# A hybrid encoder block on one core: the decay's bias moves to ScalarE, z is cut into quarter tiles among the keys, and the gating norm and spatial products go into the scans

## Chip, core and metric

The kernel runs on one core of a Trainium2 chip. The metric is device time in microseconds. A core has five instruction queues, each worked off in order: TensorE (PE, matmuls), VectorE (DVE), ScalarE (ACT), GpSimd (POOL) and SyncE (SP, which here issues most DMAs). They run beside each other and wait for each other by semaphores.

## What is computed

One layer on x, 1024 tokens by 1024 features, all in float32:

```python
x = x + 0.5 * swiglu(rmsnorm(x), ffn1)                   # 2816 hidden
p = rmsnorm(x) @ w_in                                    # u, v, q|k|v, z, b, a
y_a = gelu(u) * (W_s @ layernorm(gelu(v)) + b_s)         # 8 groups of 64, blocks of 128
q, k, v = split(silu(causal_conv4(qkv)))                 # 4 heads of 128, chunks of 64
decay = exp(where(tri, g_i - g_j, -inf))                 # g: cumulated in the chunk
L = strict(k_beta k^T * decay);  sol = (L + 1)^-1 [v_beta, k_beta e^g]
per chunk: v_new = u - w S;  o = q_dec S + attn v_new;  S = S e^gl + k_dec^T v_new
y_b = rmsnorm(o) * silu(z)
x = x + [y_a, y_b] @ w_out
x = x + 0.5 * swiglu(rmsnorm(x), ffn2);  y = rmsnorm(x)
```

## The kernel before

Matmuls keep float32's precision by splitting each operand into a high and a low part (`split`, L61 casts on ACT, L62 subtracts on DVE) and making three matmuls of it (`mm3`, L53). The two feed-forward parts form combinations of blocks (Strassen's way) on DVE and POOL. Between them lies the middle, in this order:

1. Token-major projections in token tiles of 128 (`token_steps`): eight contraction blocks, so 24 matmuls of 128x256 for a tile, into a PSUM bank `mm` (three of these), then an evacuation. First half of v (`v0`, spilled to DRAM), with the decay among it.
2. `decay(h)` for four heads: per head and half, `grb` is the row of cumulated g broadcast over partitions (a DMA), `gc` the same as a column. EL is exp(mask - grb + gc), EA is exp(grb - gc + mask), each 128x512 for four blocks of tokens: two operations on DVE (or POOL for half of EL), L900 to L905, then one Exp on ACT, L904 or L906.
3. `keys(h)`: projection and convolution of k (`proj_steps`: 24 matmuls of 128x512 into `mm` for each half, a copy to `pad` on ACT, L972, four operations on DVE, L974 and L976, a Silu on ACT, L978), then for each half four transposes (L947) and four products, L and the scaled keys to DRAM. `fill` runs two whole tiles of z's second half (`wz1`) behind each projection, 48 matmuls. There are two pads.
4. `substitute`: the 32x32 diagonal blocks of all chunks are inverted by forward substitution, 31 pairs of small DVE operations (L1023, L1025), the result X and its transpose Zb go to DRAM and are loaded again as Z and X.
5. Second half of v (`tm("v", 1, ev_v)`): gelu, layernorm (`mix`: two statistics operations on DVE, an add on DVE, a power on POOL, two scalings on DVE, L1180 to L1187), and, a pair of tiles later, `spatial`: eight matmuls of 128x128 into each of two `ax` banks, an add on DVE each (L1197).
6. Convolutions of blocks 8 and 0 (v and q of head 0), the first inverses, then eight scans of four steps each (`stage`), in which projections, inverses and queries of the next head fill PE (`weave`). Then u, the output projection, the last feed-forward part and the final norm.

A norm is one Square on ACT with a sum (L74), a multiply and add on DVE (L76), a power -0.5 on POOL (L70, `rpow`) and a scaling on DVE (L82). In the entries of the feed-forward parts its result is transposed by PE (L95) and combined (L118 and L119 casts and differences, with some L119 on POOL).

The order on each engine is not written out: a list scheduler with its own costs sets it when the program is built, by the order of the code and by what is ready. The number of buffers of each tile name limits how far it can go ahead; `tc.issue_after(ins)` holds instructions behind `ins` on their engine.

Of the kernel before, what the change touches and what calls it, by code (L numbers as in the profile page):

```python
# [30 lines left out]
def block_kernel(ctx: ExitStack, tc, a, out):  # L31
# [37 lines left out]
    def rpow(o, i, w):  # L69
        nc.gpsimd.tensor_tensor(o, i, half[:, :w], op=ALU.pow)  # L70

    def rstd_of(src, junk, n):
        ms = sm.tile([P, 1], F32, tag="ms", name="ms", bufs=4)
        nc.scalar.activation(junk, src, AF.Square, accum_out=ms)  # L74
        rs = sm.tile([P, 1], F32, tag="rs", name="rs", bufs=4)
        nc.vector.tensor_scalar(rs, ms, 1.0 / n, EPS, op0=ALU.mult, op1=ALU.add)  # L76
# [519 lines left out]
    with ExitStack() as f2:  # L596
# [150 lines left out]
        def fin(t, xt):  # L747
            o = gp.tile([P, D], F32, tag="gsp", name="o", bufs=8)
            if t < 7:
                normed(xt, st["gf"], o)  # L750
                nc.sync.dma_start(odram[t], o)
                return

            halves = slice(0, 512), slice(512, D)
# [26 lines left out]
def middle(tc, nc, a, L):  # L781
# [4 lines left out]
    bank, mm, mm3, split, rpow = L["bank"], L["mm"], L["mm3"], L["split"], L["rpow"]  # L786
# [4 lines left out]
    def K(i):  # L791
        return csa[:, i - 1]
# [95 lines left out]

    def decay(h):
        EL[h], EA[h] = (xp.tile([P, 2, 512], F32, tag="x", name="E") for _ in range(2))  # L890
        for hf in range(2):
            cs = slice(h * 8 + hf * 4, h * 8 + hf * 4 + 4)
            grb = lv.tile([P, 512], F32, tag="VT", name="grb", bufs=4)
            nc.sync.dma_start(grb, grd[:, cs.start * P:cs.stop * P].to_broadcast([P, 512]))
            lv_, av_ = v4(EL[h][:, hf]), v4(EA[h][:, hf])
# [6 lines left out]
            eng.tensor_tensor(lv_, mask(C_ML), v4(grb), op=ALU.subtract)
            eng.tensor_tensor(lv_, lv_, b4(gc[:, cs]), op=ALU.add)
            nc.scalar.activation(lv_, lv_, AF.Exp)  # L904
            nc.vector.tensor_tensor(av_, av_, mask(C_MA), op=ALU.add)  # L905
            nc.scalar.activation(av_, av_, AF.Exp)  # L906
# [81 lines left out]
    def keys(h, fill):  # L988
        kst = [kp.tile([P, 3, 512], F32, tag="kst", name="kst", bufs=3) for _ in range(2)]
        proj_conv(4 + h, [k[:, 0] for k in kst])  # L990
        for _ in range(2):
            next(fill, None)
        for hf in range(2):
            KT, kd, rw = (kst[hf][:, i] for i in range(3))
            cs = slice(h * 8 + hf * 4, h * 8 + hf * 4 + 4)
            kps = fourT(lambda t: KT[:, tl(t)])
            ssk = small("ssk")
            for t in range(4):
                nc.scalar.activation(rw[:, tl(t)], kps[:, tl(t)], AF.Square, accum_out=ssk[:, t:t + 1])
# [12 lines left out]
            nc.sync.dma_start(full(Ld, h * 2 + hf), v4(Lm))  # L1012

    def substitute():
        Lb = xp.tile([P, 32, 32], F32, tag="x", name="Lb")
        nc.sync.dma_start(Lb, diag(Ld))
        X = kp.tile([P, 32, 32], F32, tag="kst", name="X", bufs=3)
        nc.scalar.dma_start(X, a["i32"].to_broadcast([P, 1024]).rearrange("p (r c) -> p r c", r=32))
        tb = big("aT", 2)
        for j in range(31):  # L1020
            n, w = 31 - j, j + 1
            tv = tb[:, :n * w].rearrange("p (n w) -> p n w", w=w)
            nc.vector.tensor_tensor(tv, Lb[:, j + 1:, j:j + 1].to_broadcast([P, n, w]),  # L1023
                                    X[:, j:j + 1, :w].to_broadcast([P, n, w]), op=ALU.mult)
            nc.vector.tensor_tensor(X[:, j + 1:, :w], X[:, j + 1:, :w], tv, op=ALU.subtract)  # L1025
        nc.sync.dma_start(xz_d[0], X.rearrange("p r c -> p (r c)"))
        Z = xp.tile([P, 32, 32], F32, tag="x", name="Zb")
        nc.vector.tensor_copy(Z, X.rearrange("p r c -> p c r"))
# [174 lines left out]
    def ev_v(gm, later):  # L1203
        def f(t, ps):
            if t % 2 == 0:
                Vt[t // 2] = kp.tile([P, 2, 512], F32, tag="kst", name="vm", bufs=3)
                v = Vt[t // 2][:, :, 0:256]
                nc.sync.dma_start(v, sp["v"][t:t + 2, :, 0:256].rearrange("t p n -> p t n"))
                nc.scalar.activation(v, v, GELU)
            Vs = Vt[t // 2]  # L1210
            nc.scalar.activation(Vs[:, t % 2, 256:512], ps[:, :256], GELU)
            mix(t, Vs[:, t % 2], gm)
            if t % 2 == 1:
                for g in later:
                    g()
                later[:] = [partial(spatial, t, Vs, gm)]
        return f
# [77 lines left out]
    for h in range(HEADS):  # L1295
        x, y = H[h]
        if h + 1 < HEADS:
# [19 lines left out]
                wv = load_qkv(10 + h)  # L1317
            else:
                u0 = steps("u", 0, ev_u0, part=2)
            stage(x, weave(first(), queries(), (1,) + (2,) * 8), 2)  # L1320
            ny.load()
            if h + 2 < HEADS:
                wq_ = load_qkv(h + 2)
                more = proj_steps(10 + h, wv, values_of(h + 2))
            else:
                more = islice(u0, 16)
            stage(y, weave(second(), more, (1, 1, 2, 2, 2, 2, 2, 2, 2)), 2)
        else:
            stage(x, weave(chain(y.values(), y.queries()), islice(u0, 8), (0, 1, 1, 1, 0)), 1.5)
            stage(y, u0, 1)  # L1330
# [79 lines left out]
```

## Time and profile before

| | |
|---|---|
| median of three runs | 1840.59 us (1839.88 to 1841.27) |
| profiled execution, own time | 1839.26 us |
| its span | 1837.5 us |
| PE busy in the span | 1774.4 us, 97% |
| DVE, ACT, POOL busy | 1201.7, 694.2, 802.3 us |
| mean granted PE clock | 0.987 |

Views of the profile: the page gives busy time by engine; the list of waits gives what PE waited for; windows give busy time and PE's granted clock by stretch; a timeline gives each instruction or run of like instructions with its start, its duration, the idle time before it and what ended that (`[2.87 <-ACT pad L972]`); the list by lines groups instructions (count, busy us, mean ns, idle before). A name such as `pad<-mm` is what is written and what is read.

Stages by the clock of the span: first feed-forward part to about 640, keys of the four heads from 727 to 815, second half of v with the substitution from 815 to 895, scans from about 903, entry of the last feed-forward part at about 1185 to 1205.

### The profile page before, as it was taken

The page shows a single profiled execution, that of the slowest core. Times are in us where ns is not written, and L with a number is a line of the kernel's source. Part 1 is how long each engine was busy: PE and PEld are TensorE (multiplying, and loading weights), DVE is VectorE, ACT ScalarE, POOL GpSimd, SP SyncE. Part 2 cuts the span into 40 slices and gives each one's busy share as a digit, 9 for nine tenths or more (in the row PEclk, how much of TensorE's full clock was granted, in tenths as well). Part 3 has the DMA queues.
Part 4 walks back from the last instruction along what each step waited for, and adds up shares of the span by engine and source line. Part 5 has one row for each costly group of instructions (what it writes and reads, how often), then busy time and mean ns, then how long its engine had stood idle before and what let it go on. Part 6 is the DMA issues. An engine that isn't in the chain of part 4 may idle for free. (4 is left out here: it accounts for less than half of the span.)

```text
span 1837.5 us, 24764 instructions
## 1 busy us (share of the span) xinstructions
PE 1774.4 (97%) x9303; PEld 1498.3 (82%) x9303; DVE 1201.7 (65%) x1531; ACT 694.2 (38%) x1209; POOL 802.3 (44%) x627
## 2 busy tenths in 40 slices
PE   5999999999999999898999989989999999999997
PEld 4888888888888889797788978778888888888886
DVE  6867767655666585668755346797676766656546
ACT  6333233332434454332344543543333333243434
POOL 4656656665173013312132455386565665414001
PEclk8999999999999999999999999989999999999999
DMA  4254443454888554353432344324444445476744
GB/s 185 97 182 152 150 166 132 170 174 164 323 310 309 189 185 155 120 199 102 141 87 67 92 142 162 127 97 177 169 169 145 145 165 176 156 273 251 253 134 149
DMA packets 140552, 309.57 MB, mean 168 GB/s; under 512 B 27888, under 2 KB 42512, under 8 KB 140432
## 3 DMA queue, kind: packets, MB, share of 16 engines
q1 hardware_dynamic: 137936, 303.54, 47.9%
q10 hardware_dynamic: 2496, 4.44, 0.8%
q8 instruction: 73, 1.20, 0.3%
q14 instruction: 47, 0.39, 0.1%
HBM read 211.98 MB, written 95.96 MB: 168 GB/s over the span
## 5 line engine op out<-in xcount | busy, mean ns | idle before, releaser
L53 PE MATMUL mm<-unit 128*128 128x512 f32 x1056 | 242.9, 390 | 0.9 <-DVE unit L62 0.8
L53 PEld LDWEIGHTS mm<-unit 128*128 128x128 f32 x1056 | 197.6, 188 | 42.9 <-DVE unit L62 2.2
L62 DVE TENSOR_TENSOR gs<-s,gs 128x512 fp32r<-128x512 f32 x168 | 174.0, 1038 | 48.8 <-ACT gs L61 47.1
L61 ACT CAST gs<-s 128x512 fp32r<-128x512 f32 x168 | 104.1, 621 | 226.4 <-PE mm L53 111.2
L193 POOL TENSOR_TENSOR s<-graw 128x512 f32<-128x512 f32 x84 | 123.9, 1476 | 144.4 <-DMA graw<-in_f1gu_dram 112.2
L53 PE MATMUL ax<-T,gs 128*128 128x512 f32 x792 | 183.2, 389 | 0.0
L62 DVE TENSOR_TENSOR ga<-graw,ga 128x512 fp32r<-128x512 f32 x134 | 145.7, 1090 | 56.6 <-ACT ga L61 55.6
L53 PE MATMUL ax<-unit 128*128 128x512 f32 x792 | 180.5, 389 | 0.0
L53 PEld LDWEIGHTS ax<-T,gs 128*128 128x128 f32 x792 | 148.9, 188 | 31.0
L62 DVE TENSOR_TENSOR unit<-left,unit 128x1024 fp32r<-128x1024 f32 x84 | 106.8, 1272 | 103.0 <-ACT unit L61 103.0
L53 PEld LDWEIGHTS ax<-unit 128*128 128x128 f32 x792 | 148.7, 188 | 30.8
L53 PE MATMUL mm<-B,ga 128*128 128x512 f32 (+1 forms) x864 | 166.1, 346 | 3.8 <-ACT B L118 2.4
L53 PE MATMUL mm<-T,gs 128*128 128x512 f32 x720 | 166.4, 389 | 0.0
L53 PEld LDWEIGHTS mm<-B,ga 128*128 128x128 f32 x864 | 138.8, 192 | 24.0 <-ACT B L118 3.2
L53 PEld LDWEIGHTS mm<-T,gs 128*128 128x128 f32 x720 | 135.1, 188 | 28.1
L61 ACT CAST unit<-left 128x1024 fp32r<-128x1024 f32 x84 | 82.5, 982 | 191.2 <-PE ax L53 95.9
L53 PE MATMUL mm<-actT,wk 128*128 128x512 f32 x576 | 151.8, 405 | 0.0
L61 ACT CAST ga<-graw 128x512 fp32r<-128x512 f32 x134 | 83.1, 622 | 131.2 <-PE mm L53 46.0
L53 PE MATMUL ax<-B,ga 128*128 128x512 f32 x528 | 128.6, 393 | 1.7 <-DVE ga L62 1.7
L62 DVE TENSOR_TENSOR unit<-right,unit 128x1024 fp32r<-128x1024 f32 x84 | 111.2, 1324 | 27.0 <-ACT unit L61 27.0
L53 PE MATMUL mm<-wk,actT 128*128 128x256 f32 x960 | 123.8, 285 | 3.7 <-ACT pad L972 2.9
L70 POOL TENSOR_TENSOR rs<-rs,half 128x1 f32<-128x1 f32 (+1 forms) x29 | 19.4, 672 | 246.3 <-DVE rs L76 246.2
(252 smaller groups left out, 3125.0 us busy)
## 6 DMA issues: line engine op xcount, KB each, us to landing
left<-hq SPq DMA_DIRECT2D x70, 512.0 KB, 6.1
graw<-in_f1gu_dram SPq DMA_DIRECT2D x44, 512.0 KB, 5.6
wq<-t SPq DMA_DIRECT2D x44, 512.0 KB, 2.8
hq<-s SPq DMA_DIRECT2D x44, 512.0 KB, 3.1
graw<-in_f2gu_dram SPq DMA_DIRECT2D x44, 512.0 KB, 3.9
right<-wq SPq DMA_DIRECT2D x40, 512.0 KB, 4.6
wd<-in_f1wd_dram SPq DMA_DIRECT2D x22, 512.0 KB, 6.6
hq<-sg SPq DMA_DIRECT2D x22, 512.0 KB, 3.7
```

What stands on the lines that cost most here:

```text
L53: nc.tensor.matmul(*args, **kw)
L61: nc.scalar.copy(h, src)
L62: nc.vector.tensor_tensor(l, src, h, op=ALU.subtract)
L70: nc.gpsimd.tensor_tensor(o, i, half[:, :w], op=ALU.pow)
L193: nc.gpsimd.tensor_tensor(f, u, v, op=op)
```

## The change

- **Decay.** One operation adds the mask to (or takes from it) `grb`; gc, or its negative `ngc`, comes in as the bias of the Exp, a value per partition, so that each token block needs its own: 64 Exps of 128x128. Those of EL are written with the decay, those of EA behind the keys of their head. 14 of the 16 mask operations are on DVE, two on POOL.
- **z.** `part=4`: a tile of z is two steps of 12 matmuls. They stand ahead of the transposes of each half, in numbers by head and half.
- **Norms.** The multiply goes into the scale of the Square, the add to POOL, next to the power (`rsqrt`).
- **v.** `ev_v` only makes the gelu and stores it. `mixing` loads it, makes the layernorm (held behind the substitution's last operation, `solved`) and the spatial products, in steps that `beside` puts among the scans' fillers. Its constants have tiles of their own.
- **First convolutions.** Blocks 8 and 0 are held behind `solved`; their weights are loaded ahead of that.
- **Final norm.** Tile 6's scaling and store are deferred, the halves of the last tile exchanged.

```diff
+    def rsqrt(o, i, add, w=1):
+        nc.gpsimd.tensor_scalar(o, i, add, None, op0=ALU.add)
+        rpow(o, o, w)
...
-        nc.scalar.activation(junk, src, AF.Square, accum_out=ms)
+        nc.scalar.activation(junk, src, AF.Square, scale=n ** -0.5, accum_out=ms)
...
-        nc.vector.tensor_scalar(rs, ms, 1.0 / n, EPS, op0=ALU.mult, op1=ALU.add)
-        rpow(rs, rs, 1)
+        rsqrt(rs, ms, EPS)
...
+    ngc = na
+    nc.vector.tensor_scalar(ngc, gc, -1.0, None, op0=ALU.mult)
...
-            nc.vector.tensor_tensor(av_, v4(grb), b4(gc[:, cs]), op=ALU.subtract)
-            eng = nc.vector if hf else nc.gpsimd
-            eng.tensor_tensor(lv_, mask(C_ML), v4(grb), op=ALU.subtract)
-            eng.tensor_tensor(lv_, lv_, b4(gc[:, cs]), op=ALU.add)
-            nc.scalar.activation(lv_, lv_, AF.Exp)
-            nc.vector.tensor_tensor(av_, av_, mask(C_MA), op=ALU.add)
-            nc.scalar.activation(av_, av_, AF.Exp)
+            for e, i, eng, op in ((EL[h], C_ML, nc.gpsimd if hf == 0 and h < 2 else nc.vector, ALU.subtract), (EA[h], C_MA, nc.vector, ALU.add)):
+                eng.tensor_tensor(v4(e[:, hf]), K(i).unsqueeze(1).to_broadcast([P, 4, P]), v4(grb), op=op)
+
+    def exponents(e, bias, h):
+        for hf in range(2):
+            for t in range(4):
+                c = h * 8 + hf * 4 + t
+                nc.scalar.activation(e[h][:, hf, tl(t)], e[h][:, hf, tl(t)], AF.Exp, bias=bias[:, c:c + 1])
...
-        for _ in range(2):
-            next(fill, None)
         for hf in range(2):
+            for _ in range(((3, 3), (1, 3), (1, 2), (1, 2))[h][hf]):
+                next(fill, None)
...
-            rk = inv_norm(ssk, 1.0, EPS, "k")
+            rk = small("rk")
+            rsqrt(rk, ssk, EPS, 4)
...
+    def mixing(gm):
+        for t in range(0, 8, 2):
+            Vs = wp.tile([P, 2, 512], F32, tag="vm", name="vs", bufs=2)
+            nc.sync.dma_start(Vs, sp["v"][t:t + 2].rearrange("t p n -> p t n"))
+            for i in range(2):
+                with tc.issue_after(solved.ins):
+                    mix(t + i, Vs[:, i], gm)
+                yield
+            spatial(t + 1, Vs, gm)
+            yield
...
-    fill = token_steps([a["wz1"][0], a["wz1"][1]], 256, spill("z", 1), hT)
+    fill = token_steps([a["wz1"][0], a["wz1"][1]], 256, spill("z", 1), hT, part=4)
     for h in range(HEADS):
         keys(h, fill)
+        exponents(EA, ngc, h)
...
-    substitute()
+    solved = substitute()
     gm = gm_consts()
-    later = []
-    tm("v", 1, ev_v(gm, later))
+    tm("v", 1, ev_v)
+    w8, w0 = load_qkv(8), load_qkv(0)
...
+    def beside(steps):
+        for i, s in enumerate(steps):
+            if i in (1, 4, 7):
+                next(mixed, None)
+            yield s
...
-    proj_conv(8, values_of(0))
-    later.pop()()
-    proj_conv(0, queries_of(0))
+    with tc.issue_after(solved.ins):
+        together(proj_steps(8, w8, values_of(0)))
+        together(proj_steps(0, w0, queries_of(0)))
...
-            stage(x, weave(first(), queries(), (1,) + (2,) * 8), 2)
+            stage(x, weave(beside(first()), queries(), (1,) + (2,) * 8), 2)
...
-            stage(y, weave(second(), more, (1, 1, 2, 2, 2, 2, 2, 2, 2)), 2)
+            stage(y, weave(beside(second()), more, (1, 1, 2, 2, 2, 2, 2, 2, 2)), 2)
```

Three places show what the scheduler makes of it. The line numbers of the changed kernel are 4 to 12 higher than those of the kernel before. First, ACT in the keys of head 0: `E` are the decay's exponentials (in place), `wk` the weights' cast, `pad<-mm` the copy that frees PE's bank, `kst<-acc` the Silu of the keys. Before:

```order
L904 ACTIVATE E<-E 128x512 x2
L906 ACTIVATE E<-E 128x512
L836 COPY ev<-mm 128x256
L61 CAST wk<-raw 128x1024
L904 ACTIVATE E<-E 128x512
L906 ACTIVATE E<-E 128x512
L904 ACTIVATE E<-E 128x512
L906 ACTIVATE E<-E 128x512 x2
L972 COPY pad<-mm 128x512
L904 ACTIVATE E<-E 128x512
L978 ACT_TABLE_LOAD
L978 ACTIVATE kst<-acc 128x512
```

After, the same stretch and the next rows:

```order
L61 CAST wk<-raw 128x1024
L979 COPY pad<-mm 128x512
L913 ACTIVATE E<-E,na 128x128 x12
L985 ACT_TABLE_LOAD
L985 ACTIVATE kst<-acc 128x512
L979 COPY pad<-mm 128x512
L61 CAST wk<-raw 128x1024
L913 ACT_TABLE_LOAD
L913 ACTIVATE E<-E,na 128x128 x3
L1006 ACTIVATE kst,ssk<-ax 128x128 x4
L985 ACT_TABLE_LOAD
L985 ACTIVATE kst<-acc 128x512
```

The exponentials of EL (bias `gc`) are all ahead of these rows; those of EA (bias `na`, which holds `ngc`) stand around the copies and Silus of the keys, with a table load at each change between Exp and Silu. Second, DVE from the substitution's first operations on: `X<-X,aT` and `aT<-Lb,X` are the substitution, `vm` is v in its layernorm, `bst`, `bmv` and `brs` its statistics. Before:

```order
L1025 TENSOR_TENSOR X<-X,aT 128x29x3
L1197 TENSOR_TENSOR vm<-ax,bs 128x4x2x64
L1023 TENSOR_TENSOR aT<-Lb,X 128x112
L1180 BN_STATS bst<-vm 128x6
L1025 TENSOR_TENSOR X<-X,aT 128x28x4
L1182 BN_AGGR bmv<-bst 128x2
L1180 BN_STATS bst<-vm 128x6
L1023 TENSOR_TENSOR aT<-Lb,X 128x135
L1184 TENSOR_SCALAR brs<-bmv 128x1
L1186 SCALAR_TENSOR_TENSOR vm<-vm,bmv,rv 128x512
L1025 TENSOR_TENSOR X<-X,aT 128x27x5
L1187 SCALAR_TENSOR_TENSOR vm<-vm,brs,rv 128x512
```

After, at the substitution's end:

```order
L1031 TENSOR_TENSOR aT<-Lb,X 128x60
L1033 TENSOR_TENSOR X<-X,aT 128x2x30
L1031 TENSOR_TENSOR aT<-Lb,X 128x31
L1033 TENSOR_TENSOR X<-X,aT 128x31
L981 TENSOR_SCALAR acc<-pad,cw 128x512
L1036 COPY Zb<-X 128x1024
L983 SCALAR_TENSOR_TENSOR acc<-pad,cw,acc 128x512
L981 TENSOR_SCALAR acc<-pad,cw 128x512
L983 SCALAR_TENSOR_TENSOR acc<-pad,cw,acc 128x512 x4
L1192 BN_STATS bst<-vs 128x6
```

Layernorm, spatial adds and convolutions have left the substitution, in which only three `L62 TENSOR_TENSOR wk<-raw,wk` remain, and stand behind its last operation. Third, POOL at the entry of the last feed-forward part: `rs` is a norm's scale, `T` a combination's low part, `s` a sum of weights. Before:

```order
L119 TENSOR_TENSOR T_10404<-f,T_10404 128x4x128
L70 TENSOR_TENSOR rs<-rs,half 128x1 x3
L119 TENSOR_TENSOR T_10408<-f,T_10408 128x4x128
L119 TENSOR_TENSOR T_10708<-f,T_10708 128x4x128 x2
L193 TENSOR_TENSOR s_10734<-graw 128x512
L70 TENSOR_TENSOR rs<-rs,half 128x1
L193 TENSOR_TENSOR s_10736<-s_10734,graw 128x512
```

After:

```order
L74 TENSOR_SCALAR rs<-ms 128x1
L70 TENSOR_TENSOR rs<-rs,half 128x1
L163 TENSOR_TENSOR f<-f 128x512
L123 TENSOR_TENSOR T_10453<-f,T_10453 128x4x128
L74 TENSOR_SCALAR rs<-ms 128x1
L70 TENSOR_TENSOR rs<-rs,half 128x1
L74 TENSOR_SCALAR rs<-ms 128x1
L70 TENSOR_TENSOR rs<-rs,half 128x1
L123 TENSOR_TENSOR T_10449<-f,T_10449 128x4x128
L123 TENSOR_TENSOR T_10453<-f,T_10453 128x4x128
L123 TENSOR_TENSOR T_10753<-f,T_10753 128x4x128 x2
L197 TENSOR_TENSOR s_10779<-graw 128x512
```

The fourth power, which stood behind four rows of T and s, now stands ahead of them, next to its add.

More of the change, by code (lines that the diff above doesn't have):

```diff
@@ L749, in fin, with scaled @@
             if t < 7:
[L750 to L754, printed above, removed]
+                rs = rstd_of(xt, o, D)
+                def scaled():
+                    nc.vector.scalar_tensor_tensor(o, xt, rs, st["gf"], op0=ALU.mult, op1=ALU.mult)
+                    nc.sync.dma_start(odram[t], o)
+                if t == 6:
+                    return scaled
+                return scaled()
+            halves = slice(512, D), slice(0, 512)
             ms = sm.tile([P, 2], F32, tag="ms2", name="ms2")
@@ L757, in fin @@
             for i, f in enumerate(halves):
-                nc.scalar.activation(o[:, f], xt[:, f], AF.Square, accum_out=ms[:, i:i + 1])
+                nc.scalar.activation(o[:, f], xt[:, f], AF.Square, scale=D ** -0.5, accum_out=ms[:, i:i + 1])
             nc.gpsimd.tensor_tensor(rs, ms[:, 0:1], ms[:, 1:2], op=ALU.add)
-            nc.gpsimd.tensor_scalar(rs, rs, 1.0 / D, EPS, op0=ALU.mult, op1=ALU.add)
-            rpow(rs, rs, 1)
+            rsqrt(rs, rs, EPS)
             for f, eng in zip(halves, (nc.sync, nc.scalar)):
@@ L785, in middle @@
     hT, ident, sp, ba = L["hT"], L["ident"], L["sp"], L["ba"]
-    bank, mm, mm3, split, rpow = L["bank"], L["mm"], L["mm3"], L["split"], L["rpow"]
+    bank, mm, mm3, split, rpow, rsqrt = L["bank"], L["mm"], L["mm3"], L["split"], L["rpow"], L["rsqrt"]
     csa = kp.tile([P, NCONST - 1, P], F32, tag="kst", name="csa", bufs=3)
@@ L894, in decay @@
             nc.sync.dma_start(grb, grd[:, cs.start * P:cs.stop * P].to_broadcast([P, 512]))
-            lv_, av_ = v4(EL[h][:, hf]), v4(EA[h][:, hf])
-            def mask(i):
-                return K(i).unsqueeze(1).to_broadcast([P, 4, P])
-            nc.vector.tensor_tensor(av_, v4(grb), b4(gc[:, cs]), op=ALU.subtract)
-            eng = nc.vector if hf else nc.gpsimd
-            eng.tensor_tensor(lv_, mask(C_ML), v4(grb), op=ALU.subtract)
-            eng.tensor_tensor(lv_, lv_, b4(gc[:, cs]), op=ALU.add)
-            nc.scalar.activation(lv_, lv_, AF.Exp)
-            nc.vector.tensor_tensor(av_, av_, mask(C_MA), op=ALU.add)
-            nc.scalar.activation(av_, av_, AF.Exp)
+            for e, i, eng, op in ((EL[h], C_ML, nc.gpsimd if hf == 0 and h < 2 else nc.vector, ALU.subtract), (EA[h], C_MA, nc.vector, ALU.add)):
[5 more added lines that the diff above has]
+                nc.scalar.activation(e[h][:, hf, tl(t)], e[h][:, hf, tl(t)], AF.Exp, bias=bias[:, c:c + 1])
     Zt, Xt = [], []
@@ L1024, in substitute @@
                                     X[:, j:j + 1, :w].to_broadcast([P, n, w]), op=ALU.mult)
-            nc.vector.tensor_tensor(X[:, j + 1:, :w], X[:, j + 1:, :w], tv, op=ALU.subtract)
+            last = nc.vector.tensor_tensor(X[:, j + 1:, :w], X[:, j + 1:, :w], tv, op=ALU.subtract)
         nc.sync.dma_start(xz_d[0], X.rearrange("p r c -> p (r c)"))
@@ L1029, in substitute @@
         nc.sync.dma_start(xz_d[1], Z.rearrange("p r c -> p (r c)"))
+        return last
     class Half:
@@ L1163, in gm_consts, with const @@
     def gm_consts():
-        lng, lnb = big("rv", 2), big("rv", 2)
+        def const():
+            return wp.tile([P, 512], F32, tag="gmc", name="gmc", bufs=4)
+        lng, lnb = const(), const()
         nc.scalar.dma_start(lng, a["gm_ln_g"].to_broadcast([P, 512]))
@@ L1170, in gm_consts @@
         for i in range(2):
-            w = v4(big("u", 2))
+            w = v4(const())
             nc.scalar.dma_start(w, a["gmw"][:, i * 512:i * 512 + 512].rearrange("p (g n) -> p g n", g=4))
@@ L1201, in spatial, with ev_v @@
         nc.sync.dma_start(sp["m"][t - 1:t + 1].rearrange("t p n -> p t n"), Vs)
[L1203 to L1217, printed above, removed]
+    def ev_v(t, ps):
+        if t % 2 == 0:
+            Vt[t // 2] = kp.tile([P, 2, 512], F32, tag="kst", name="vm", bufs=3)
+            v = Vt[t // 2][:, :, 0:256]
+            nc.sync.dma_start(v, sp["v"][t:t + 2, :, 0:256].rearrange("t p n -> p t n"))
+            nc.scalar.activation(v, v, GELU)
+        nc.scalar.activation(Vt[t // 2][:, t % 2, 256:512], ps[:, :256], GELU)
+        if t % 2 == 1:
+            nc.sync.dma_start(sp["v"][t - 1:t + 1].rearrange("t p n -> p t n"), Vt[t // 2])
+    def mixing(gm):
[8 more added lines that the diff above has]
+            yield
     def ev_u0(t, ps):
@@ L1243, in middle @@
         decay(h)
+        exponents(EL, gc, h)
         together(islice(v0, 2))
-    fill = token_steps([a["wz1"][0], a["wz1"][1]], 256, spill("z", 1), hT)
+    fill = token_steps([a["wz1"][0], a["wz1"][1]], 256, spill("z", 1), hT, part=4)
     for h in range(HEADS):
         keys(h, fill)
+        exponents(EA, ngc, h)
     together(fill)
-    substitute()
+    solved = substitute()
     gm = gm_consts()
-    later = []
-    tm("v", 1, ev_v(gm, later))
+    tm("v", 1, ev_v)
+    w8, w0 = load_qkv(8), load_qkv(0)
     H = [[Half(h, hf) for hf in range(2)] for h in range(HEADS)]
@@ L1272, in weave @@
         yield from few
+    mixed = mixing(gm)
+    def beside(steps):
[3 more added lines that the diff above has]
+            yield s
     def stage(x, filler, rate):
```

## The prediction

> **What bounds the kernel now.** The page comes first: how long the span is and how much of it TensorE (PE) works.
>
> ```profile
> span 1837.5 us, 24764 instructions
> PE 1774.4 (97%) x9303; PEld 1498.3 (82%) x9303; DVE 1201.7 (65%) x1531; ACT 694.2 (38%) x1209; POOL 802.3 (44%) x627
> ```
>
> PE is busy 97% of the time, and the change takes no matmul away (it cuts some groups smaller and moves others). So it can only win what PE waits, about 60 us in all, and what PE loses to a low clock behind a wait. The second view is the list of PE's waits by what ended them (columns: us in all, times, longest).
>
> ```profile
> PE ax L95 <- DVE B L119: 10.8, 5, 7.0
> ...
> PE ax L53 <- DVE vm L1187: 4.4, 3, 2.9
> ```
>
> Both lie where the change works: most of the first at the entry of the last feed-forward part, the second in the second half of v, beside the substitution. A third place, the keys of head 0, has two waits of their own kind in this list; their rows follow below. The third view is the table of stretches; its seventh column is PE's granted clock.
>
> ```profile
> 903.00:1057.00 154.00, 151.99 (x1369) 130.82 (x1369) 76.57 (x170) 69.34 (x172) 51.85 (x61) 1.00 0.29 85
> 1200.00:1225.00 25.00, 23.81 (x146) 21.76 (x147) 24.31 (x29) 14.61 (x29) 21.19 (x15) 0.86 0.30 97
> ```
>
> In the scans (903 to 1057) PE has nothing to win, 152 of 154 us, and VectorE (DVE) is half free; at the entry PE's clock falls to 0.86. The fourth view, the timeline, says why.
>
> **Keys of head 0.** PE's rows, in order (start, duration, instruction, idle before):
>
> ```profile
> 727.63 10.84 PE L53 MATMUL mm<-actT,wk 128*128 128x512 f32 x47
> ...
> 740.80 1.56 PE L53 MATMUL mm<-wk,actT 128*128 128x256 f32 x11 [0.81 <-DVE wk L62]
> 745.24 4.63 PE L53 MATMUL mm<-wk,actT 128*128 128x256 f32 x24 [2.87 <-ACT pad L972]
> ...
> 755.10 0.66 PE L947 MATMUL ax<-ident,kst 128*128 128x128 f32 x4 [3.53 <-ACT kst L978]
> ...
> 756.59 12.38 PE L53 MATMUL mm<-actT,wk 128*128 128x512 f32 x47
> 768.80 5.82 PE L53 MATMUL mm<-wk,actT 128*128 128x256 f32 x48
> ```
>
> Idle: 0.81 + 2.87 + 3.53 = 7.2 us. Slow running: the x24 took 4.63 where half of the x48 is 2.91, so 1.7; the x47 after the second gap took 12.38 against 10.84, so 1.5. Together 10.5 us. What made ScalarE (ACT) late stands in the rows of GpSimd (POOL) and ACT:
>
> ```profile
> 719.25 1.82 POOL L902 TENSOR_TENSOR E<-csa,grb 128x512 f32<-128x512 f32 x1 [5.17 <-issue]
> ...
> 732.88 9.01 POOL L902 TENSOR_TENSOR E<-csa,grb 128x512 f32<-128x512 f32 x1 [4.05 <-DMA grb<-grd]
> ```
>
> ```profile
> 743.04 0.63 ACT L904 ACTIVATE E<-E 128x512 f32<-128x512 f32 x1 [5.82 <-POOL E L903]
> 743.58 1.13 ACT L906 ACTIVATE E<-E 128x512 f32<-128x512 f32 x2
> 744.62 0.56 ACT L972 COPY pad<-mm 128x512 f32<-128x512 f32 x1
> ```
>
> One POOL operation took 9.01 us instead of 1.82 while DVE ran one decay operation after another, and the copy that frees PE's bank stood behind an exponential that needed it. Afterwards this operation is no longer on POOL (only heads 0 and 1, first halves, stay there), and DVE has 14 decay operations where it had 24. At the 0.68 us of a DVE row here that is 9.5 us from 719.2 on, and a microsecond or two for the two operations that still run on POOL beside it: done near 730, not 739.6 (738.94 + 0.68).
>
> ```profile
> 738.94 0.68 DVE L903 TENSOR_TENSOR E<-E,gc 128x512 f32<-128x512 f32 x1
> ```
>
> What ACT gets instead is 64 exponentials of 128x128 for 16 of 128x512. No row shows this form. From below: an L906 costs 0.51 in a row (1.13 less 0.62), so a quarter at least 0.13; from above, the nearest ACT row with a per-partition operand and this tile:
>
> ```profile
> L1130 ACT ACTIVATE oh<-sq,ex 128x128 f32<-128x128 f32 x32 | 11.8, 368 | 16.7 <-PE sq L53 16.3
> L978 ACT ACT_TABLE_LOAD x2 | 2.6, 1283 | 0.0
> ```
>
> I take 0.26: its 0.37 less the 0.11 by which neighbours overlap in L906. That is 64 x 0.26 = 16.6 us against 16 x 0.51 = 8.2, 8 us more on an engine that is 38% busy. Exponentials also now stand between Silus, so tables (1.28 us each) are loaded five times in keys of head 0, three of them ahead of the second Silu. Walked along the queue: 32 exponentials end near 730.5, cast, 8 more, cast, copy of the first half at 735.5 (744.6 before), 12 more, table, Silu at 740.3; copy, cast, table, 3 more, 4 squares, table, second Silu done at 747. PE, no longer idle, with 36 z matmuls ahead of each half's transposes (4.3 us each by the x48), wants the first Silu at 742.5 and the second at 748.2. Both fit, the second by a microsecond: all 10.5 us go. At 0.37 per exponential both would be late by 1 to 1.5 us.
>
> By the Trainium skill, "ScalarE: Activation LUTs", What ACT_TABLE_LOAD costs, a switch takes 1.28 us plus a drain of 1.38, 2.66 in all, and a [128,1] bias pointer makes an ACTIVATE 280 ns plus 0.833 per element; by that the second Silu would be near 752 and PE some 4 us late. This trace has the 1283 ns; no row here shows the drain. It speaks against the change, and is the second rival's case.
>
> Heads 2 and 3 have only 12 and 24 z matmuls ahead of their halves' transposes: 24 x 0.12 = 2.9 us and some 2.7 of transposes and products against copy, four convolution operations, Silu and hand-overs of about 6: +0.35 each, **+0.7** (0 to 2).
>
> **v and the substitution.**
>
> ```profile
> 815.52 14.73 PE L53 MATMUL mm<-wk,actT 128*128 128x256 f32 x123
> ...
> 831.82 2.02 PE L53 MATMUL ax<-vm,u 128*128 128x128 f32 x16 [0.99 <-issue]
> ...
> 841.50 3.65 PE L53 MATMUL ax<-vm,u 128*128 128x128 f32 x16 [2.95 <-DVE vm L1187]
> ...
> 894.99 0.41 PE L53 MATMUL ax<-Z,L 32*32 32x32 f32 x8 [0.36 <-DMA Z<-xz]
> ```
>
> ```profile
> 831.98 0.21 DVE L1023 TENSOR_TENSOR aT<-Lb,X 128x31 f32<-128x31 f32 x1 [0.26 <-DMA Lb<-Ld]
> 832.22 0.22 DVE L1025 TENSOR_TENSOR X<-X,aT 128x31 f32<-128x31 f32 x1
> ...
> 885.47 1.11 DVE L1028 COPY Zb<-X 128x1024 f32<-128x1024 f32 x1
> ```
>
> ```profile
> L1025 DVE TENSOR_TENSOR X<-X,aT 128x31 f32<-128x31 f32 (+15 forms) x31 | 10.4, 335 | 0.3
> L1023 DVE TENSOR_TENSOR aT<-Lb,X 128x31 f32<-128x31 f32 (+15 forms) x31 | 10.4, 334 | 0.5 <-DMA Lb<-Ld 0.3
> L62 DVE TENSOR_TENSOR wk<-raw,wk 128x1024 fp32r<-128x1024 f32 x4 | 4.8, 1212 | 0.2 <-ACT wk L61 0.2
> L1187 DVE SCALAR_TENSOR_TENSOR vm<-vm,brs,rv 128x512 f32<-128x512 f32 x8 | 5.9, 750 | 2.3 <-POOL brs L70 2.2
> L1180 DVE BATCH_NORM_STATS2 bst<-vm 128x6 f32<-128x512 f32 x8 | 5.3, 676 | 4.0 <-ACT vm L1209 4.0
> L1197 DVE TENSOR_TENSOR vm<-ax,bs 128x512 f32<-128x512 f32 x8 | 5.4, 677 | 1.4 <-PE ax L53 1.4
> ```
>
> PE waited 4.4 for the layernorm, 1.0 and 0.36, and ran the 3.65 us group 1.6 too long: 7.4 us, gone with the spatial products. The substitution took 53.5 us (831.98 to 885.5) for 20.8 of own work. Alone it takes 20.8 + 62 hand-overs of 0.03 + three splits of 1.21 = 26.3. From the end of the last key products (815.5, call it zero) its input landed at 16.5; with DVE freer by some 2 us sooner, which I estimate as 14. Its end is then at 40.5, the copy at 41.6, and the way out and back to PE is as before, 894.99 less 886.6 = 8.4: the inverse can begin at 50. PE has 189 matmuls of 0.12 and 108 of 0.226 until then, 47.0: it waits 3 us, and may lose 1.7 of clock after it as after the 2.87 us gap. Net -7.4 + 3.2 + 1.7 = **-2.5** (-7.4 if the wait vanishes, +2 if the input lands no sooner and the convolutions, whose pads hold PE's banks until behind the substitution, add to it).
>
> The clock's part, by rows: gaps of 2.87 and 2.95 were already followed by matmuls at half speed. The Trainium skill, "TensorE: Matmul & The Clock Gate", Part 1: The HAM clock gate, has the clock fall after at least one idle window of about 3.4 us; by that the coming 3 us wait would cost no clock and the sum would be 1.7 lower. These rows speak otherwise.
>
> **Scans.** Eight layernorms (0.68 + 2 x 0.75 + small) and eight adds of 0.68, 26 us, and some convolutions come to DVE there: from 77 to about 110 of 160 us. The spatial matmuls are the same work elsewhere. DVE has the room, but each operation is in line with the steps of the recurrence: **+1.5** (0 to 5). The gelu of v now goes out and comes back in eight more transfers on SP's queue; the 16 DMA engines are 29% busy in the scans (the 0.29 of that row) and the loads stand two or more steps ahead of their use, so I count them at nothing; if one came late, DVE would stop at that layernorm, the same mechanism as the slower rival below.
>
> **Entry of the last feed-forward part.**
>
> ```profile
> 1200.22 1.08 PE L95 MATMUL ax<-ident,xn 128*128 128x128 f32 x4 [7.03 <-DVE B L119]
> ...
> 1205.51 12.08 PE L53 MATMUL mm<-B,ga 128*128 128x256 f32 x94
> ```
>
> ```profile
> 1186.98 4.71 DVE L82 SCALAR_TENSOR_TENSOR xn<-x,rs,grow 128x1024 f32<-128x1024 f32 x3 [0.45 <-POOL rs L70]
> 1191.62 0.14 DVE L76 TENSOR_SCALAR rs<-ms 128x1 f32<-128x1 f32 x1
> ...
> 1196.27 2.28 DVE L82 SCALAR_TENSOR_TENSOR xn<-x,rs,grow 128x1024 f32<-128x1024 f32 x1 [2.88 <-POOL rs L70]
> ```
>
> ```profile
> 1188.64 5.86 POOL L119 TENSOR_TENSOR T<-f,T 128x512 fp32r<-128x512 f32 x3
> ...
> 1195.68 0.55 POOL L70 TENSOR_TENSOR rs<-rs,half 128x1 f32<-128x1 f32 x1
> ```
>
> The fourth norm's scale stood on DVE behind three long L82, so its power came behind 7.0 us of other POOL work (1188.64 to 1195.68). Now POOL does add and power itself, and all four pairs stand ahead of that work: the fourth L82 ends near 1191 to 1193, not 1198.5, and PE transposes 6 us earlier. The next operands then come late in turn (DVE is 24.3 of 25 us busy there), so I count not 7 but **-5.5** (-1 to -9). Other norms: start -0.4, and +0.3 for the add that POOL now does before each power on short chains (two small POOL operations where one was; the last tile's order of halves and the deferred store of tile 6 change only what stands beside each other, bounds -0.5 to +0.5).
>
> **Sum:** -10.5 + 0.7 - 2.5 + 1.5 - 5.5 - 0.4 + 0.3 = -16.4. The profiled execution took 1839.26 us (1.8 outside its span); the median of the runs is 1.33 above. 1839.26 - 16.4 + 1.33 = **1824**. A measurement of this kernel tells 0.2%, 3.7 us, from no change.
>
> **The rivals.**
> - The entry stays bound (chance 0.18): DVE, full there, makes PE wait for other operands, -1 for -5.5, and the scans give back 5 for 1.5: 1832. For it: 24.3 of 25 us; against: the 7 us have one named cause that goes.
> - ACT becomes late in keys of head 0 (0.10): table switches and small exponentials delay each Silu, PE loses 4 us idle and 1.7 of clock: 1830. For: five loads; against: 9 us of room gained ahead of them.
> - Slower (0.09): in the scans DVE stops at each layernorm's last operation until POOL's power is there, with the recurrence's u and S updates behind it. POOL holds products of 1.0 to 1.4 us there and a power of 1.1; a wait of 3.5 behind all of them, eight times, is 28 us, so 1824 - 1.5 + 28 = 1850. It decides from 16.4 / 8 = 2 us per layernorm on, where the gain is gone, and is a measured loss from 2.5. Against: before, eight such waits (last L1187 column) were 2.3 us in all.
> - All stalls vanish (0.09): no wait at the inverse (-7.4), entry -9, scans 0: 1814.
> - The forecast itself 0.54.
>
> The range 1812 to 1837 holds all but the slower rival and the tails of two others. Faster by over 0.2%: the four cases on that side, 0.91, less 0.04 for their tails above 1837, so 0.87; within: that 0.04 and 0.01 of the slower rival, 0.05; slower: 0.08.
>
> **What would show it.** Right: no PE idle over 1 us in keys of head 0, the first pad copy near 735; the substitution in about 26 us, then a PE wait of about 3 us ended by the DMA of Z; scans over 98% busy; PE's wait at the entry under 2 us. Wrong: PE waiting for u or S in the scans, a Silu late behind a table load, or a span that shrinks by under 10 us.

## The result, and the profile after

The changed kernel takes 1829.17 us (median of four runs, 1829.02 to 1831.51) against 1840.93 of the kernel before on the same chip: ratio 0.9949, 95% interval 0.9931 to 0.9968. A second set of runs (e8 below) gave 0.9953 (0.9939 to 0.9967). So it is faster by 9 to 12 us. The forecast was 1824, 16.6 faster, range 1812 to 1837: the sign and the range hold, the sum is 5 to 7 us too large.

The page of the profiled execution (span, then busy time by engine), and PE's list of waits:

```profile
span 1829.6 us, 24826 instructions
...
PE 1775.9 (97%) x9303; PEld 1498.5 (82%) x9303; DVE 1203.4 (66%) x1487; ACT 709.1 (39%) x1261; POOL 801.5 (44%) x656
```

```profile
PE ax L99 <- DVE x L86: 14.2, 5, 9.5
PE ax L99 <- DVE B L123: 6.2, 6, 2.3
...
PE ax L53 <- issue: 2.9, 1, 2.9
PE ax L99 <- DVE B L148: 2.7, 2, 2.4
...
PE mm L53 <- DVE unit L62: 2.6, 3, 1.9
...
PE ax L954 <- ACT kst L985: 1.1, 2, 0.8
```

The layernorm's wait of 4.4 is gone, the keys' 6.4 (behind ACT) became 1.1, the 11.3 behind combined operands, mostly the entry's, became 6.2 + 2.7. But the waits for a norm (behind L82 and L76 before, behind L86 after) grew from 13.1 to 15.3, and a wait of 1.95 behind `unit` is new. Two profiled executions of each kernel (the second of before is e9, of after e8), cut at the same matmuls of PE:

| stretch of PE, us | before | after | forecast | measured (means) |
|---|---|---|---|---|
| start to first key projection | 727.4, 726.5 | 730.4, 731.2 | -0.1 | +3.8 |
| to the last key products | 87.3, 84.7 | 78.1, 78.2 | -9.8 | -7.9 |
| to the second u projection (192 matmuls) | 242.8, 243.4 | 239.2, 238.8 | -1.0 | -4.1 |
| to the 62 matmuls of the output projection | 46.8, 47.6 | 48.7, 47.1 | 0 | +0.6 |
| to the 94 matmuls behind the last entry | 101.2, 100.8 | 97.8, 97.5 | -5.5 | -3.4 |
| to the last 132 matmuls into `ax` | 562.1, 563.2 | 562.9, 562.5 | 0 | 0 |
| to the span's end | 69.9, 70.7 | 72.5, 71.6 | 0 | +1.8 |

The keys of head 0 in the PE timeline after, against the rows with 2.87 and 3.53 before:

```profile
730.41 11.08 PE L53 MATMUL mm<-actT,wk 128*128 128x512 f32 x48
741.33 4.40 PE L53 MATMUL mm<-wk,actT 128*128 128x256 f32 x36
...
746.82 4.49 PE L53 MATMUL mm<-wk,actT 128*128 128x256 f32 x36
752.15 0.66 PE L954 MATMUL ax<-ident,kst 128*128 128x128 f32 x4 [0.84 <-ACT kst L985]
...
753.45 11.17 PE L53 MATMUL mm<-actT,wk 128*128 128x512 f32 x48
```

One wait of 0.84 is left, and 48 matmuls take 11.1 to 11.2 throughout. On ACT:

```profile
736.04 2.47 ACT L913 ACTIVATE E<-E,na 128x128 f32<-128x128 f32 x8
...
739.34 0.60 ACT L979 COPY pad<-mm 128x512 f32<-128x512 f32 x1
...
750.17 1.28 ACT L985 ACT_TABLE_LOAD   x1
751.46 0.63 ACT L985 ACTIVATE kst<-acc 128x512 f32<-128x512 f32 x1
```

A small exponential costs 0.30 us in a row ((2.47 less one of 0.40) / 7), not 0.26. That is what the Trainium skill, "ScalarE: Activation LUTs", What ACT_TABLE_LOAD costs, gives (280 ns + 0.833 x 128 less 93 of overlap, 0.29). Of the drain that it adds to a table load nothing is seen: the Silu starts 1.29 after the load of 1.28.

The substitution and the inverse after, on DVE and PE:

```profile
825.92 0.21 DVE L1031 TENSOR_TENSOR aT<-Lb,X 128x31 f32<-128x31 f32 x1 [10.42 <-DMA Lb<-Ld]
...
852.66 1.12 DVE L1036 COPY Zb<-X 128x1024 f32<-128x1024 f32 x1
```

```profile
831.68 24.67 PE L53 MATMUL mm<-actT,wk 128*128 128x512 f32 x108
859.27 0.49 PE L53 MATMUL ax<-Z,L 32*32 32x32 f32 x8 [2.92 <-issue]
859.70 1.65 PE L53 MATMUL mm<-actT,wk 128*128 128x512 f32 x3
...
863.79 5.06 PE L53 MATMUL mm<-actT,wk 128*128 128x512 f32 x11
...
903.17 0.96 PE L53 MATMUL mm<-actT,wk 128*128 128x512 f32 x3
```

The substitution takes 26.4 us (825.9 to 852.3; forecast 26.3). PE waits 2.9 for Z, and its next matmuls take 0.46 to 0.55 each instead of 0.23 (11 in 5.06): from 860 to 869 the granted clock is 0.50, and 1.00 again from 870.

The norms are where the forecast has no row at all. At the hand-over from the first feed-forward part, on POOL and on DVE:

```profile
651.62 1.31 POOL L74 TENSOR_SCALAR rs<-ms 128x1 f32<-128x1 f32 x1
653.01 0.57 POOL L70 TENSOR_TENSOR rs<-rs,half 128x1 f32<-128x1 f32 x1
653.67 1.31 POOL L74 TENSOR_SCALAR rs<-ms 128x1 f32<-128x1 f32 x1
```

```profile
651.57 1.28 DVE L86 SCALAR_TENSOR_TENSOR xn<-x,rs,grow 128x1024 f32<-128x1024 f32 x1 [0.77 <-POOL rs L70]
653.62 1.28 DVE L86 SCALAR_TENSOR_TENSOR xn<-x,rs,grow 128x1024 f32<-128x1024 f32 x1 [0.77 <-POOL rs L70]
655.67 1.29 DVE L86 SCALAR_TENSOR_TENSOR xn<-x,rs,grow 128x1024 f32<-128x1024 f32 x1 [0.77 <-POOL rs L70]
```

POOL's add of 128 numbers takes 0.22 us where DVE is idle (0.22 at 5.98), and 1.31 here: it ends with DVE's scaling of the norm before. Only then comes the power, 0.57, and DVE waits 0.77 for it, idle. So the norms of this chain follow each other at 2.05 us, of which DVE works 1.28. The same place before, on POOL and on DVE:

```profile
649.53 1.46 POOL L70 TENSOR_TENSOR rs<-rs,half 128x1 f32<-128x1 f32 x1 [1.46 <-DVE rs L76]
```

```profile
651.02 1.28 DVE L82 SCALAR_TENSOR_TENSOR xn<-x,rs,grow 128x1024 f32<-128x1024 f32 x1 [0.44 <-POOL rs L70]
652.29 0.68 DVE L103 TENSOR_TENSOR actT<-ax,actT 128x512 fp32r<-128x512 f32 x1
653.04 1.28 DVE L82 SCALAR_TENSOR_TENSOR xn<-x,rs,grow 128x1024 f32<-128x1024 f32 x1
```

There the scalings are no closer (2.02 us here), but DVE does other work between them. From the first of the four scalings to the end of the last it is 8.8 us before and 10.4 after. And a power of 1.46, beside a DVE split of 1.22, already showed that a small POOL operation can stretch.

### The profile page after: what moved, and what is told of

Its sections match the earlier page's. It is cut to its first block, busy times and chain, and to the rows that moved or that the text cites. A ratio compares the mean times of both kernels' runs of the same rounds, so it can differ in the third digit from the quotient of the medians.

```text
span 1829.6 us, 24826 instructions
## 1 busy us (share of the span) xinstructions
PE 1775.9 (97%) x9303; PEld 1498.5 (82%) x9303; DVE 1203.4 (66%) x1487; ACT 709.1 (39%) x1261; POOL 801.5 (44%) x656
## 5 line engine op out<-in xcount | busy, mean ns | idle before, releaser
L62 DVE TENSOR_TENSOR gs<-s,gs 128x512 fp32r<-128x512 f32 x168 | 178.5, 1064 | 49.3 <-ACT gs L61 47.3
L62 DVE TENSOR_TENSOR ga<-graw,ga 128x512 fp32r<-128x512 f32 x134 | 143.8, 1075 | 52.8 <-ACT ga L61 52.0
L62 DVE TENSOR_TENSOR unit<-left,unit 128x1024 fp32r<-128x1024 f32 x84 | 106.9, 1274 | 105.0 <-ACT unit L61 104.9
L62 DVE TENSOR_TENSOR unit<-right,unit 128x1024 fp32r<-128x1024 f32 x84 | 111.3, 1325 | 26.8 <-ACT unit L61 26.8
L53 PEld LDWEIGHTS mm<-actT,wk 128*128 128x128 f32 x576 | 104.9, 192 | 19.3
```

The source lines that it names most:

```text
L53: nc.tensor.matmul(*args, **kw)
L62: nc.vector.tensor_tensor(l, src, h, op=ALU.subtract)
```

## Experiments

The theory after the result: decay and v bring what the table shows; the norms' add on POOL takes about 6 us back at the start, the hand-over and the end, and gives 3.4 at the last entry. The rival: those 6 us are the schedule's, or due to transfers that came late by chance. All ratios are to the kernel before on the same chip, with 95% intervals.

**e1: the add back on DVE.**

```diff
-        nc.scalar.activation(junk, src, AF.Square, scale=n ** -0.5, accum_out=ms)
+        nc.scalar.activation(junk, src, AF.Square, accum_out=ms)
...
-        rsqrt(rs, ms, EPS)
+        nc.vector.tensor_scalar(rs, ms, 1.0 / n, EPS, op0=ALU.mult, op1=ALU.add)
+        rpow(rs, rs, 1)
...
-            rk = small("rk")
-            rsqrt(rk, ssk, EPS, 4)
+            rk = inv_norm(ssk, 1.0, EPS, "k")
```

> The changed kernel with the norms' multiply and add back on VectorE (and the keys' add too); all else as changed. Theory (GpSimd's add in a norm is slow while VectorE works, 1.1 to 1.3 us for 0.22, and VectorE waits 0.77 us for each power): the start is 0.9 us and the hand-over to the middle 2.1 us shorter, and the last 3 us of waiting before the final matmuls go, but the wait at the entry of the last feed-forward part comes back (3.4 us): about 2.6 us faster than the changed kernel, 1826.5. Rival (those losses are the schedule's or a late transfer's, not the add's): only the entry's gain is lost, 3.4 us slower than the changed kernel, 1832.5.

Measured: 1825.11 us, 0.9909 (0.9876 to 0.9942). The first key projection starts at 726.0, the last stretch takes 69.9, the entry 101.5, and the four scalings at the hand-over take 8.8 us again: the places moved as the theory has them. The time is 4 us under the changed kernel's, but these runs were on another chip, and the two intervals of the ratio just touch (0.9942 and e8's 0.9939). The pair on one chip is e5, below, which leaves the add on POOL only at the last entry, against e8: 1822.94 (1821.30 to 1825.33) against 1829.07 (1828.66 to 1829.38), 6.1 us, the theory's 6.

The end shows how far a norm reaches. After, on ACT, DVE and PE (o is the final norm's scaling, `left` an operand of the last products, of which ACT casts the high part and DVE makes the low part):

```profile
1795.04 1.05 ACT L61 CAST unit<-left 128x1024 fp32r<-128x1024 f32 x1 [0.96 <-DMA left<-hq]
```

```profile
1798.01 1.29 DVE L757 SCALAR_TENSOR_TENSOR o<-x,rs,grow 128x1024 f32<-128x1024 f32 x1 [0.77 <-POOL rs L70]
1799.21 1.22 DVE L62 TENSOR_TENSOR unit<-left,unit 128x1024 fp32r<-128x1024 f32 x1
```

```profile
1800.48 20.52 PE L53 MATMUL mm<-unit 128*128 128x512 f32 x82 [1.95 <-DVE unit L62]
```

The operand had landed and was cast at 1795.04. But its low part stands in DVE's queue behind three of the final norm's scalings, each of which waits 0.77 for POOL. So it starts at 1799.21, and PE waits 1.95. In e1 the last of these scalings starts at 1792.64, the low part at 1793.84, and PE has:

```profile
1795.11 18.92 PE L53 MATMUL mm<-unit 128*128 128x512 f32 x82 [0.37 <-DVE unit L62]
```

Before, too, these 82 took 18.88 behind a wait of 0.37. (On SP's queue three loads go out behind the norms' stores, at 1799.69; their operands are cast from 1804.29 on, and PE does not wait for them.)

**e2: the norm change alone on the kernel before.** e1's diff the other way round, on before (there `nc.gpsimd.tensor_scalar(rs, ms, EPS, None, op0=ALU.add)` and the power).

> The kernel before with the norm change alone (scale in the Square, add on GpSimd). Theory: +0.9 at the start, +2.1 at the hand-over, +3.2 at the end, -3.4 at the last entry: 2.8 us slower than before, 1843.7. Rival (the add costs nothing): 3.4 us faster than before, 1837.5.

Measured: 1839.98 us, 0.9999 (0.9977 to 1.0021). That is no change, with an interval of -4.2 to +3.9 us, which holds both numbers: the time decides nothing. The places do: first projection at 728.5 (+1.5), entry 98.4 (-2.7), end 72.4 (+2.1), each the way that the theory has it and smaller.

**e3: the decay alone; e4: z in quarters alone; e9: the kernel before again.** e3 takes the decay's lines of the diff over, and

```diff
         decay(h)
+        exponents(EL, gc, h)
...
         keys(h, fill)
+        exponents(EA, ngc, h)
```

e4 takes over the z lines:

```diff
-    fill = token_steps([a["wz1"][0], a["wz1"][1]], 256, spill("z", 1), hT)
+    fill = token_steps([a["wz1"][0], a["wz1"][1]], 256, spill("z", 1), hT, part=4)
...
+            for _ in range(((3, 3), (1, 3), (1, 2), (1, 2))[h][hf]):
+                next(fill, None)
```

> The kernel before with the decay's change alone (one mask operation, bias in 64 small exponentials). Theory (GpSimd's 9 us operation was the cause, and z in quarters only covers the second Silu): the first wait in keys of head 0 goes, before the second half's transposes 2.4 us and a clock loss of 1.7 stay, because table loads and exponentials stand ahead of the second Silu: 6.4 us faster than before, 1834.5. Rival (the decay alone does all): 10.5 us faster, 1830.4.

> The kernel before with z in quarter tiles alone. Theory: the first Silu is as late as before and PE, with fewer matmuls ahead of it, waits about 7 us once instead of 6.4 in two; one clock loss of 1.5 goes, 0.7 comes in heads 2 and 3: about 1 us faster than before, 1840, no change that can be told. Rival (more even filling hides most of the lateness): 5 us faster, 1836.

Measured: e3 1832.37 us, 0.9964 (0.9938 to 0.9989), 6.6 us, as expected; keys 78.1 us with one wait of 1.79 for the second Silu. e4 1836.40 us, 0.9971 (0.9949 to 0.9993), 5.3 us with an interval of 1.3 to 9.4, and 2.1 by the medians (1838.53 before): too wide to tell the theory's 1 from the rival's 5. Keys take 82.7 us with one wait of 2.90. In e4 GpSimd's operation that had taken 9.01 us took 1.52, and the first Silu came 2.4 us earlier than before, so the expectation's ground was gone. e9 asked whether that operation matters:

> The kernel before, unaltered, for a second look at keys of head 0. Theory (the 9 us operation on GpSimd is not what bounds that place: VectorE's 24 decay operations ahead of the weight split and the convolution do; in two kernels above it took 1.5 to 1.7 us and the waits of 2.7 and 3.5 us were still there): whether it takes 9 or 1.6 us here, the keys' stretch from the first projection to the last products is 85.5 to 87.5 us. Rival (the long operation makes the waits): with a short one the stretch is under 82 us.

Measured: 1838.75 us (a single run). The operation took 1.55, and the waits were there:

```profile
731.74 1.55 POOL L902 TENSOR_TENSOR E<-csa,grb 128x512 f32<-128x512 f32 x1 [3.77 <-DMA grb<-grd]
```

```profile
740.03 0.68 DVE L903 TENSOR_TENSOR E<-E,gc 128x512 f32<-128x512 f32 x1
740.64 1.21 DVE L62 TENSOR_TENSOR wk<-raw,wk 128x1024 fp32r<-128x1024 f32 x1
```

```profile
741.90 5.93 PE L53 MATMUL mm<-wk,actT 128*128 128x256 f32 x35 [2.76 <-DVE wk L62]
...
751.65 0.66 PE L947 MATMUL ax<-ident,kst 128*128 128x128 f32 x4 [2.24 <-ACT kst L978]
```

Keys took 84.7 us, just under the expected 85.5 and far over 82. So most of the wait was DVE's decay operations, which have z's weight split behind them. They end 14.2 us behind the start of the first key projection here (14.1 in e2, 14.3 in e4, short operation too), and 12.2 behind it with the long operation, before and in e7 (below), where it was long again:

```profile
731.23 9.21 POOL L902 TENSOR_TENSOR E<-csa,grb 128x512 f32<-128x512 f32 x1 [4.46 <-DMA grb<-grd]
```

With it long, keys take 87.3 us both times; with it short, 84.7 here and 85.8 in e2 (1.66 there). POOL's 9 us so add 1.5 to 2.6. Against e9, e4's quarters make the keys 2.0 shorter.

**e7: the v part alone on the kernel before** (mixing, beside, solved and the first convolutions of the diff; no line of decay, z or norms).

```diff
-    tm("v", 1, ev_v(gm, later))
+    tm("v", 1, ev_v)
+    w8, w0 = load_qkv(8), load_qkv(0)
```

> The kernel before with the v part alone: layernorm and spatial products in the scans, first convolutions behind the substitution. Theory: from the end of the keys to the u projection 3.6 us less, as in the changed kernel, and nothing elsewhere: 3.6 us faster than before on the same chip. Rival (the stretch is short only because the keys end earlier and leave VectorE free): no gain.

Measured: 1832.89 us, 0.9974 (0.9961 to 0.9987), 4.8 us (2.4 to 7.2), which holds the expected 3.6. The stage itself won twice that: from keys' end to the u projection it took 235.4 us, 7.4 less than before and 3.6 less than in the changed kernel. The wait for Z was 1.62, and what follows was soon at full speed (granted clock 0.50 from 864 to 867.3):

```profile
863.49 0.41 PE L53 MATMUL ax<-Z,L 32*32 32x32 f32 x8 [1.62 <-DMA Z<-xz]
863.83 1.95 PE L53 MATMUL mm<-actT,wk 128*128 128x512 f32 x4
...
867.94 2.55 PE L53 MATMUL mm<-actT,wk 128*128 128x512 f32 x10
```

**e8: the changed kernel again.**

> The changed kernel once more, unaltered, for another look and a time on this chip. Theory: about 0.5% under before, and the wait of about 1.9 us ahead of the final matmuls is there again, since the final norms cause it. Rival (that wait was one late transfer): it is gone, and the profiled time is near 1826.5.

Measured: 1829.07 us, 0.9953 (0.9939 to 0.9967), profiled at 1828.9 with a span of 1826.8. The wait of 1.95 ahead of the final matmuls is there again, so it is not chance. What differs between the two executions is PE's clock: the 82 matmuls behind that wait take 19.62 instead of 20.52, and the output projection 47.1 instead of 48.7.

**e5 and e11: the add on POOL only at the last entry; e6: a filler in the wait for Z; e10: whole z tiles.** e5 is e1 with `normed(xs[i + 4 * j], g2, xns[i][j], pool=True)`, which selects the changed kernel's scale and `rsqrt` for these four norms alone.

> As e1 (add on VectorE), but the four norms whose power stood behind GpSimd's other work at the entry of the last feed-forward part keep scale in the Square and add on GpSimd. Theory (the two effects are separate places): e1's 1825.1 less the entry's 3.3: 1821.8, about 7 us faster than the changed kernel. Rival (at the entry the gain hung on the other norms too): no better than e1, 1825.

> The kernel of e5 again, unaltered, as the pair of e10 on one chip: 1823, about 0.8% under before.

Measured: e5 1822.94 us, 0.9921 (0.9906 to 0.9936); e11 1823.42 us, 0.9915 (0.9901 to 0.9928). The entry takes 99.0 and 98.8 us against e1's 101.5. e5 beats both kernels; that it beats e1 too (1825.11, an interval that overlaps) isn't shown by the times. e6 adds to e5:

```diff
+    fl = bank(ps_s, "sq")
+    for _ in range(6):
+        mm(fl, ident, Xs.rearrange("p r c -> p (r c)")[:, 0:512], start=True, stop=True)
```

> As e5, with six matmuls of 128x512 more, whose result nobody uses, that read the substitution's result and so run just ahead of the wait for Z; the schedule moves 12 projection matmuls (2.7 us) behind the first inverse for them. Theory (the 2.9 to 3.4 us wait for Z costs a low clock for some 8 us behind it, about 3.9 us): the clock stays at 1, the run of 11 projection matmuls in the inverse takes 2.5 us instead of 4.3, and the whole is 1.2 us faster than e5. Rival (these matmuls are slow because of what stands between them, not the clock): the durations stay, 2.7 us slower than e5.

Measured: 1829.44 us, 0.9955 (0.9939 to 0.9971), 6.5 slower than e5: worse than either number. The filler did take the wait for Z away, and three matmuls behind it run at full speed (0.96); but a wait of 4 us comes one step later:

```profile
855.67 0.41 PE L53 MATMUL ax<-Z,L 32*32 32x32 f32 x8 [0.49 <-DMA Z<-xz]
856.01 0.96 PE L53 MATMUL mm<-actT,wk 128*128 128x512 f32 x3
860.95 0.60 PE L53 MATMUL ax<-rv,X 32*32 32x32 f32 x8 [3.99 <-POOL pad L979]
...
863.20 2.93 PE L53 MATMUL mm<-actT,wk 128*128 128x512 f32 x6
```

The releaser named had long been done. On ACT the copy of rv, which that product reads, started at 860.62, behind a Silu:

```profile
860.08 0.63 ACT L989 ACTIVATE wq<-acc 128x512 f32<-128x512 f32 x1 [3.23 <-DVE acc L987]
860.62 0.24 ACT L1074 COPY rv<-ax 32x128 f32<-32x128 f32 x1
```

So the convolutions that are held behind the substitution stand, through ACT's queue, in front of the inverse; the wait for Z had hidden that. A shorter filler was not tried. e10 is e5 with e4's lines undone:

> As e5, with z in whole tiles behind each projection, as before. Theory (the quarters win 1 us in the keys, 77.2 against 78.1 us from first projection to last products, and take nothing elsewhere): 1 us slower than e5. Rival (with whole tiles the wait for Z is 1.6 us and the slow stretch behind it short, as in e7): 1 us lost in the keys, 3.3 won at the inverse, 2.3 us faster than e5.

Measured: 1823.29 us, 0.9921 (0.9907 to 0.9936): the same as its pair e11, and not to be told from the theory's +1; the rival's 2.3 faster is not seen, though each stage moved the rival's way. Keys take 80.2 us instead of 77.2, and from the inverse to the u projection 184.8 instead of 188.4. The inverse in e10, then in e11:

```profile
856.77 0.41 PE L53 MATMUL ax<-Z,L 32*32 32x32 f32 x8 [1.81 <-DMA Z<-xz]
...
859.78 2.59 PE L53 MATMUL mm<-actT,wk 128*128 128x512 f32 x10
```

```profile
855.16 0.60 PE L53 MATMUL ax<-Z,L 32*32 32x32 f32 x8 [2.63 <-issue]
...
859.78 5.06 PE L53 MATMUL mm<-actT,wk 128*128 128x512 f32 x11
```

With the decay done, the quarters win 0.9 to 3.0 us in the keys (e3, whole tiles as well, has 78.1) and lose 2.2 to 3.8 from the inverse on (whole tiles: 184.8, and 185.1 in e7; quarters: 187.3 to 188.6 in e1, e5, e11 and the changed kernel). The clock carries the loss: it is 1.00 throughout in e10, and 0.50 from 855 to 865 in e11.

## Why the prediction was right, and where not

- **Norms: the step that failed.** "+0.3 for the add that POOL now does before each power on short chains" and "start -0.4" were +3.8 up to the first key projection and +1.8 at the end. The term was costed by the power's row, a POOL operation that ran while DVE waited for it. The add runs beside DVE's scaling of the norm before, and stretches to its end; no row stands behind the "-0.4". e1 shows it: without the add on POOL the first projection comes 4.4 us sooner, the last stretch takes 2.6 less. e5 against e8 gives the price, 6.1 us. Of the +3.8, 1.7 to 2.0 arise at the hand-over (from the last 132 matmuls of the first part to the first key projection it is 113.7 us before, in e9 and in e1, and 115.4 to 115.6 in e2, e8 and the changed kernel). The rest arises in the first 70 us: about 1 us by later norms, the rest by a slow stretch of PE near 63 us, which one of the two executions of before has as well and e2 has not. How much of that is the add's stays open.
- **Keys, -9.8.** -9.2 against the execution that the forecast was made from, -6.5 in the other pair. The place and the cure were right; "One POOL operation took 9.01 us instead of 1.82" was the cause of 1.5 to 2.6 us only. The rest came from DVE, which the forecast's own row shows busy until 739.6 (e9).
- **v, -2.5, and scans, +1.5.** Together -4.1. The wait came as forecast (2.9 and 2.4 for 3.2), by two errors that cancel: the input landed 16.6 us behind the key products, not 14, and the way from the copy's end to PE took 5.5, not 8.4. (The forecast's own sum slips a little: 14 + 26.3 is 40.3, and 50 - 47.0 is 3.0.) The clock cost more than 1.7: 16 projection matmuls took 7.9 us for 3.6, so 4.3. The scans cost nothing: PE works 153.4 of 154 us there. With these sizes the forecast's terms, -7.4 + 2.9 + 4.3, would give -0.2. PE's idle time accounts for the difference in part: it fell from 7.75 to 3.5 us, 1.4 of it in the scans. Its busy time rose by 0.7, where the terms give 2.7; these 2 us stay open.
- **Entry, -5.5.** -3.4. The norm's wait of 7 us went, and waits of 1.5 and 2.4 for the next operands came, as forecast in kind and under-priced. e5, e11 and e2 give it alone: 2 to 3 us.
- **The slower rival** did not come: layernorm's last operation waits 1.4 us in all for POOL.
- **z in quarters** was counted as cover for the second Silu. e10 shows that, and that it then costs as much from the inverse on. In the forecast nothing joins these two places. So the parts taken alone do not add up: e3, e4 and e7 win 6.6, 2.1 to 5.3 and 4.8 us, e2 nothing, 13 to 17 in all against 9 to 12 together. Why the clock fell behind a wait of 2.63 in e11 and not behind one of 1.81 in e10 is not settled.
- **The signs.** One PE wait of 0.84 in the keys, a substitution of 26.4, a wait of 2.9 for Z and scans over 99% busy came as set. Of the waits at the entry, 1.5 and 2.4, one is over the 2 that was set. And one of the signs of being wrong came: the span shrinks by under 10 us, 7.9 in the first pair and 9.1 in the means, which points at the norms.
- **Luck.** Against the forecast, the stages are off by +3.9 (start), +1.9 (keys), -3.1 (v and scans), +0.6 (output projection), +2.1 (entry) and +1.8 (end). The v stage, better than its own terms give, pays for half of the norms' miss of 5.7.

## What to carry to other kernels

An operation on a second engine is priced by a row in which the first engine does what it will do beside it; a chain that goes to and fro between two engines is priced by its period, not by the sum of its operations. A stretched operation next to a wait is not yet its cause: another run of the same kernel, in which it is short, tells. And work that fills one wait is taken from the next one on the same chain, so stages are compared in pairs.

## What the runs showed of the hardware

- The same POOL operation on 128x512, at the same place beside DVE's decay operations, took 9.01 and 1.55 us in two executions of the kernel before, and 9.21 (e7), 1.52 (e4) and 1.66 (e2) in kernels that have the same operations there. In the long cases DVE's neighbours took 0.68 us each, in the short ones up to 1.5.
- A POOL add of 128x1 took 0.22 us alone and 1.14 to 1.31 beside a DVE operation of 1.22 to 1.28, and ended with it.
- Behind the wait for Z, PE's granted clock was 0.50 for 3.3 us after a wait of 1.62 (e7), and for 6 to 10 us of thin work (32x32 products between single projection matmuls) after waits of 2.35 to 3.70 (the changed kernel, e8, e11, e1, e5); after one of 1.81 (e10) it stayed at 1.00. The Trainium skill, "TensorE: Matmul & The Clock Gate", Part 1: The HAM clock gate, asks for an idle window of about 3.4 us; these runs show less. In the output projection the same wait of 2.35 was followed by half speed in one of two executions of the changed kernel, and in one of two of the kernel before.
